# S5's pk products in 64 by 64 tiles over two PSUM banks, an early touch of pb, toe and kst, and a few reordered steps

## The chip, the cores and the metric

The kernel runs on one core of one Trainium2 chip. The metric is the device time of one execution in microseconds (us). Before the change the median of three runs is 1424.18 us (1423.64 to 1424.38). One execution was profiled; its own time and its span stand in the table further down.

TensorE (PE) does the matrix products, VectorE (DVE) and ScalarE (ACT) the elementwise work, GpSimd (POOL) a few small steps, SyncE (SP) issues the DMAs. SBUF is the working memory; PSUM, in eight banks, takes the products.

## The reference

One layer of a hybrid decoder on 256 prompt positions and 8 by 8 sample positions, so 320 columns in all, in float32. What matters here:

```
proj = rms_norm(x) @ w_in                      # S5 input u | q | k | v | g
s5:  x_t = lam_bar * x_{t-1} + B_bar u_t       # 64 groups of 16 channels, 64 complex states each
     y   = Re(C x) + d * u ;  y = gelu(y) ;  y * sigmoid(y @ w_glu + b)
ret: 8 heads of 128, rotary q and k, decay per head, chunked scan, norm per head, silu(g) gate
x = x + concat(s5, ret) @ w_out
x = x + (silu(h2 @ w_gate) * (h2 @ w_up)) @ w_ffn_out
```

The outputs are the two normed activations and the final S5 and retention states.

## The kernel before

**Dense products.** Every weight matrix is streamed from HBM in tiles of 8 blocks of 128 by 128 (`wload`, L122): an SP DMA fills `raw`, ACT casts it to `hi` (L133), DVE makes the rest `lo` (L135), three buffers each. `gemm` (L139) does three products for each block, hi by xhi, hi by xlo, lo by xhi (L145 to L147), each with 320 columns. The projections (`ps_p`) come first, then the output projections, the feed-forward part and a tail.

**Order.** PE and POOL run in the order in which the program is written down (`manual_schedule`, L944). That order comes from a planner: `clk.now` is moved on by a cost for each product (0.4 a block in `gemm`, the first argument of `mm` elsewhere), `spawn` puts a generator on a heap with a due time, and `run_due`, called between the blocks of a product, emits whatever is due. So the S5 and retention steps lie between the blocks of the projections. ACT, DVE and SP are put in order by the compiler's scheduler, by readiness and priority: weight loads come first (offset 3000), then evacuations of PSUM (`EVAC`, 1500), then the rest in program order. Once built, each engine and each DMA queue runs its list strictly in order.

**S5.** Eight chunks of 8 groups (`s5_chunk`, L578). A chunk c starts at planner time T0 + 32 c. It

- copies u into `up_`, writes it to DRAM (`via`, L586) and reads it back in another layout with eight SP DMAs into `kst` (L590), two buffers, so a chunk's eight wait until the chunk two before has used its buffer in `s5_outputs`;
- makes `cl0` (tile name `cz`), the C factors in a layout with blocks of zeros, with four ACT instructions (L597), `bl` and `cl` on DVE;
- 14.2 planner units later (`b1`) has PE transpose `bl` four times into `pt` (L625), which ACT copies to `bst`;
- 6.6 units later (`b2`) emits the outputs of the chunk before (`pending.pop()()`, L632: products `py` from `toe`, `kst`, `cl` and `xp`), then 16 products `pb` from `bst` and `kst` in 64 by 64 tiles, then the 8 products `pk_` from `bl` and `cl0` in 128 by 64 tiles (L645), written to columns 320 to 383 of the first of pb's two banks;
- copies pk to the last part of `toe` (L649), from where six SP DMAs (L654) make the other three parts of `toe`, and runs the scan (`s5_scan`).

A float32 product shows as two PE instructions in the profile. The tile form stands in its row, as 128\*128, 64\*64 or 128\*64 (rows by columns of the array).

**Retention, head 0.** `finish_norm` scales the rotary table and releases `s5_params2` (six DVE steps, L419), which waits behind the table's second product (`turned`, L997). `do_q` (L876) rotates q (`rot_`) and makes `qg` (two DVE products, L893). `do_k` (L900) rotates k. `head_k` transposes k, `head_v` transposes v, makes `vT`, copies a part of it to `vsp` (L770) and, for odd heads, uses it in `po`.

**Start.** POOL builds `ident`, then sets `ones` (L64), which eight warming products on PE use. 

Of the kernel before, what the change touches and what calls it, by code (L numbers as in the profile page):

```python
# [12 lines left out]
F32 = mybir.dt.float32  # L13
# [7 lines left out]
P = 128  # L21
# [11 lines left out]
CH = 4  # L33
NCP = NP // CH
NC = N // CH
# [11 lines left out]
def hybrid_kernel(ctx, tc, xT, w_in, w_in4, w_out, w_glu, w_fi, w_fo, w_fot, gfr, vecs, s5p, bc, x0,  # L47
# [11 lines left out]


    ident = cst.tile([P, P], F32, name="ident")
    make_identity(nc, ident)
    ones = cst.tile([P, P], F32, name="ones")
    pool.memset(ones, 1.0)  # L64
    mhalf = cst.tile([P, 4], F32, name="mhalf")
    pool.memset(mhalf, -0.5)
    vec = cst.tile([P, vecs.shape[1]], F32, name="vec")
# [251 lines left out]

    d0s = [s5.tile([P, 2, 4, NCP], F32, name=f"d0{i}") for i in range(2)]  # L320
    xps = [s5.tile([P, 2, 4, NC], F32, name=f"xp{i}") for i in range(2)]
    cl0s = [s5.tile([P, 2, 4, 32], F32, name=f"cz{i}") for i in range(2)]

    cls_ = [s5.tile([P, 2, 4, CH, 16], F32, name=f"cl{i}") for i in range(2)]


    toe = s5.tile([P, 4, CH, 16], F32, name="toe")
    for t_ in (*d0s, *xps, toe, *cl0s):
        pool.memset(t_, 0.0)
    scr = [None, 0]  # L330

# [245 lines left out]
    def s5_chunk(c):  # L577
        js = slice(4 * c, 4 * c + 4)  # L578
        cl, cl0, xp, d0 = cls_[c % 2], cl0s[c % 2], xps[c % 2], d0s[c % 2]

        up_ = s5.tile([P, CH, NC], F32, name="up_", tag="up_", bufs=2)
        with tc.issue_after(rot_t["keys"].ins) if c < 2 else nullcontext():
            act.copy(up_, u32[:, c].rearrange("p (c s) -> p s c", s=CH))

        via = drm.tile([4, 2, 16, CH, NC], F32, name="via", tag="via", bufs=2)
        sp.dma_start(via.rearrange("j g h s c -> (j g h) (s c)"), up_.rearrange("p s c -> p (s c)"))  # L586
        kst = s5.tile([P, 4, NC], F32, name="kst", tag="kst", bufs=2)
        for i in range(2):
            for e in range(CH):
                sp.dma_start(kst[64 * i + 16 * e:64 * i + 16 * e + 16],  # L590
                             via[2 * i:2 * i + 2, :, :, CH - 1 - e].rearrange("q g h c -> h (q g) c"))

        raw = raws[c]
        for q in range(2):
            for g in range(2):
                with tc.issue_after(rot_t["values"].ins):
                    act.mul(cl0[64 * g:64 * g + 64, q, :, 16 * g:16 * g + 16],  # L597
                            raw[64 * g:64 * g + 64, 1, 4 * q:4 * q + 4], 1.0 - 2.0 * q)
        with tc.issue_after(rot_t["values"].ins):
            act.copy(d0[:, :, :, 1:], r4[:, js].unsqueeze(1).unsqueeze(3).to_broadcast([P, 2, 4, NCP - 1]))  # L600
        shm = [P, 8, CH, 16]
        for w_, pc in ((0, gpc), (1, lpc)):
            m1, m2 = (s5.tile(shm, F32, name=f"m{q}", tag=f"m{q}", bufs=1) for q in range(2))
            b_ = raw[:, w_].unsqueeze(2).to_broadcast(shm)
            tt(m1, b_, pc[:, c, 0].unsqueeze(3).to_broadcast(shm), MUL)
            tt(m2, b_, pc[:, c, 1].unsqueeze(3).to_broadcast(shm), MUL)
            if w_ == 0:

                bl = s5.tile([P, 2, 2, 2, CH, 16], F32, name="bl", tag="bl", bufs=1)
                for r, (a, b, op) in enumerate(((m1[:, 0:4], m2[:, 4:8], SUB), (m1[:, 4:8], m2[:, 0:4], ADD))):  # L610
                    a, b = (t_.rearrange("p (u q) e h -> p u q (e h)", q=2) for t_ in (a, b))
                    tt(bl[:, r].rearrange("p q u e h -> p u q (e h)"), a, b, op)
                continue
            tt(cl[:, 0], m1[:, 0:4], m2[:, 4:8], SUB)
            tt(cl[:, 1], m1[:, 4:8], m2[:, 0:4], SUB)
        if c:
            tbl = s5_table(c)
        yield DL["b1"] + (4.0 if c == 0 else 0.0)
        if not c:
            tbl = s5_table(c)  # L620
        bst = s5.tile([P, 4, P], F32, name="bst", tag="bst", bufs=1)
        pt = misc("pt")
        for i in range(4):
            tr(pt[:, P * i:P * i + P], bl[:, i // 2, i % 2].rearrange("p u e h -> p (u e h)"))
        with tc.high_priority(offset=EVAC):  # L625
            act.copy(bst, pt.rearrange("p (i s) -> p i s", s=P))
        load_bc(c + 2)
        yield DL["b2"]
        if c:
            while clk.now - used["misc"] < MISC:  # L630
                yield 0.4
            pending.pop()()  # L632
        pb = ps_b.tile([P, 2, 512], F32, name="pb", tag="pb", bufs=1)
        for i in range(4):
            for u in range(2):

                for g in range(2):
                    us, gs = slice(64 * u, 64 * u + 64), slice(64 * g, 64 * g + 64)
                    mm(0.04, pb[gs, u, NC * i:NC * i + NC], bst[us, i, gs], kst[us, 2 * (i % 2) + g],
                       start=True, stop=True, tile_position=(64 * u, 64 * g))  # L640
        pk_ = pb[:, 0, 4 * NC:4 * NC + 64]
        for i in range(2):
            for q in range(2):
                for u in range(2):
                    mm(0.04, pk_[64 * u:64 * u + 64, 32 * i:32 * i + 32],  # L645
                       bl[:, q, i, u].rearrange("p e h -> p (e h)"), cl0[:, q, 2 * u + i],
                       start=q == 0, stop=q == 1, tile_position=(0, 64 * u))
        with tc.high_priority(offset=EVAC):
            act.copy(toe[:, :, CH - 1], pk_.rearrange("p (q h) -> p q h", h=16))  # L649
        with tc.high_priority(offset=4 * EVAC if c == 7 else 0):  # L650
            for u in range(2):
                for t in range(CH - 1):
                    d = 16 * (CH - 1 - t)
                    sp.dma_start(toe[64 * u + d:64 * u + 64, :, t], toe[64 * u:64 * u + 64 - d, :, CH - 1])  # L654
        with tc.high_priority(offset=2 * EVAC if c == 7 else 0):
            s5_scan(c, pb, xp, d0, tbl)
        if c < 7:
            pending.append(lambda: s5_outputs(c, kst, cl, xp))
            return
        yield DL["scan"]  # L660
        while clk.now - used["misc"] < MISC:
            yield 0.4
        s5_outputs(c, kst, cl, xp)
# [61 lines left out]
    def rot_(ps, name):  # L725
        sw = mp.tile([P, N], F32, name="sw", tag="sw", bufs=1)
        act.copy(sw[0:64], ps[64:128])
        rot_t["keys"] = act.copy(sw[64:128], ps[0:64])
        a = mp.tile([P, N], F32, name=name, tag=name, bufs=1)
        tt(a, ps, csr[:, 0], MUL)  # L730
        tt(sw, sw, csr[:, 1], MUL)
        tt(a, a, sw, ADD)
        return a

    def head_k(h, q_, qg, k_, R):
# [25 lines left out]
    def head_v(h, v_, qg, rt, R):  # L761
# [5 lines left out]
        with tc.high_priority(offset=EVAC):  # L767
            for i in range(3):
                act.mul(vT[:, i], pst2[:, P * i:P * i + P], rtok[:, i:i + 1])
        act.copy(vsp[64 * (h % 2):64 * (h % 2) + 64], vT[64:128, 2])  # L770
        last = act.copy(vs[:, h], vT[64:128, 2])
        if h == 0:
            rot_t["values"] = last
# [24 lines left out]
        with tc.high_priority(offset=GN):  # L798
            for i in range(nt):
                dve.bn_stats(st[:, i], po[:, i])  # L800
                dve.bn_aggr(mv[:, :, i], st[:, i])

        m_, t_, y_, w_ = mv[:, 0], mv[:, 1], y[:, 0], y[:, 1]
        pool.tensor_scalar(m_, m_, -1.0, None, MUL)
# [6 lines left out]
        pool.tensor_tensor(w_, m_, y_, MUL)  # L811
        if h == 0:
            rot_t["first"]()
        on = mp.tile([P, 3, P], F32, name="on", tag="on", bufs=1)

        def normed():
# [59 lines left out]
    def do_q(h, ps=None):  # L876
# [13 lines left out]
        q_ = rot(ps, "q_")  # L890
        pool.tensor_copy(qsp[:, 64 * (h % 2):64 * (h % 2) + 64], q_[:, NP:N])
        qg = qgs[h % 2]
        for u in range(2):  # L893
            tt(qg[:, u].rearrange("p (b w) -> p b w", w=40)[:, :, 0:NS],
               q_[:, NP + 32 * u:NP + 32 * u + 32].rearrange("p (b t) -> p b t", t=NS),
               gqt[:, h].unsqueeze(1).to_broadcast([P, 4, NS]), MUL)
        R.update(q_=q_, qg=qg)
        run_due()

    def do_k(h, ps=None):  # L900
        ps = proj(9 + 4 * h) if ps is None else ps
        R = HS[h]
        k_ = rot(ps, "k_")
        pool.tensor_tensor(kvf[:, h], k_[:, NP:N].rearrange("p (b t) -> p b t", t=NS),
                           kdt[:, h].unsqueeze(1).to_broadcast([P, NB, NS]), MUL)
        pool.tensor_copy(ksp[:, 64 * (h % 2):64 * (h % 2) + 64], k_[:, NP:N])
        spawn(head_k(h, R["q_"], R["qg"], k_, R))
        run_due()
# [80 lines left out]
    def finish_norm():  # L989
        next(rg)  # L990
        act.copy(rtok, ytok[0])
        yield 4.5
        rps = next(rg)
        with tc.high_priority(offset=EVAC):
            act.copy(rbc, rps)
            tt(csr[:, 0], csr[:, 0], rbc, MUL)
            turned = dve.tensor_tensor(csr[:, 1], csr[:, 1], rbc, MUL)  # L997
            tt(u32[:, 0], ps0, rbc, MUL)
            tt(u32[:, 1], ps1, rbc, MUL)
        rot_t["ready"] = True  # L1000

        with tc.issue_after(turned.ins):
            s5_params2(exps[1])

    spawn(finish_norm(), DL["nm"])

# [538 lines left out]
```

## Time and profile before

| what | value |
| --- | --- |
| median of three runs | 1424.18 us |
| profiled execution, its own time | 1424.95 us |
| its span, first to last instruction | 1423.2 us |
| ACT busy | 606.5 us (43%) |
| POOL busy | 122.8 us (9%) |
| HBM read and written | 254.44 MB and 10.52 MB |
| granted PE clock, mean | 0.999 |

The page of the profile lists busy time by engine, groups of instructions and the chain of work that ended last. Times in timelines are counted from the start of the span. A row of the timeline has start, length, engine, line, operation, the tile written and the tiles read, the form, and the number of like instructions merged in it; a bracket tells how long the engine was idle before it and what ended that. "SPq" is a DMA issue in SP's queue: its length is the issue, not the transfer. "PEld" is the loading of weights into the array.

### The profile page before, as it was taken

The page shows a single profiled execution, that of the slowest core. Times are in us where ns is not written, and L with a number is a line of the kernel's source. Part 1 is how long each engine was busy: PE and PEld are TensorE (multiplying, and loading weights), DVE is VectorE, ACT ScalarE, POOL GpSimd, SP SyncE. Part 2 cuts the span into 40 slices and gives each one's busy share as a digit, 9 for nine tenths or more (in the row PEclk, how much of TensorE's full clock was granted, in tenths as well). Part 3 has the DMA queues.
Part 4 walks back from the last instruction along what each step waited for, and adds up shares of the span by engine and source line. Part 5 has one row for each costly group of instructions (what it writes and reads, how often), then busy time and mean ns, then how long its engine had stood idle before and what let it go on. Part 6 is the DMA issues. An engine that isn't in the chain of part 4 may idle for free.

```text
span 1423.2 us, 26196 instructions
## 1 busy us (share of the span) xinstructions
PE 1415.5 (99%) x10376; PEld 1406.6 (99%) x10376; DVE 957.9 (67%) x1842; ACT 606.5 (43%) x973; POOL 122.8 (9%) x194
## 2 busy tenths in 40 slices
PE   9999999999999999999999999999999999999998
PEld 8999999999999999999999999999999999999998
DVE  7979878787557747777777545767644677655453
ACT  6654555555455443333333333333333333334553
POOL 7720111110000000100001000000000000000002
PEclk9999999999999999999999999999999999999999
DMA  8554555555644466675666446666545765445542
GB/s 278 170 187 158 163 174 157 171 163 157 218 156 151 164 209 228 221 253 201 245 206 231 136 148 238 233 216 235 170 146 175 255 233 190 159 157 184 154 143 75
DMA packets 102316, 267.07 MB, mean 188 GB/s; under 512 B 27377, under 2 KB 42033, under 8 KB 102193
## 3 DMA queue, kind: packets, MB, share of 16 engines
q1 hardware_dynamic: 101904, 265.01, 55.9%
q8 instruction: 81, 1.33, 0.4%
q10 hardware_dynamic: 288, 0.39, 0.1%
q14 instruction: 43, 0.34, 0.1%
HBM read 254.44 MB, written 10.52 MB: 186 GB/s over the span
## 4 chain that ended last, share of the span: by engine, by line
PE 96%; DVE 2%; DMA 1%; ACT 1%; issue 1%; POOL 0%; SPq 0%; POOLq 0%; DVEq 0%; ACTq 0%
PE ps_fg L147 7%; PE ps_fu L147 7%; PE ps_fu L146 7%; PE ps_fg L146 7%; PE ps_fg L145 7%; PE ps_fu L145 7%; PE ps_fo L147 7%; PE ps_fo L145 7%; PE ps_fo L146 7%; PE ps_p L145 6%; PE ps_p L147 6%; PE ps_p L146 6%; PE ps_o L145 2%; PE ps_o L146 2%; PE ps_o L147 2%; PE ps_t L1342 1%
## 5 line engine op out<-in xcount | busy, mean ns | idle before, releaser
L133 ACT CAST hi<-raw 128x1024 fp32r<-128x1024 f32 (+1 forms) x410 | 397.8, 971 | 684.2 <-PE ps_fg L146 182.3
L135 DVE TENSOR_TENSOR lo<-raw,hi 128x1024 fp32r<-128x1024 f32 (+1 forms) x410 | 462.8, 1129 | 304.2 <-ACT hi L133 301.3
L147 PE MATMUL ps_fg<-hhi,lo 128*128 128x320 f32 x704 | 218.0, 310 | 0.0
L147 PE MATMUL ps_fu<-hhi,lo 128*128 128x320 f32 x704 | 217.9, 310 | 0.0
L145 PE MATMUL ps_fg<-hhi,hi 128*128 128x320 f32 x704 | 217.9, 310 | 0.0
L146 PE MATMUL ps_fu<-hlo,hi 128*128 128x320 f32 x704 | 217.9, 310 | 0.0
L145 PE MATMUL ps_fu<-hhi,hi 128*128 128x320 f32 x704 | 217.9, 310 | 0.0
L146 PE MATMUL ps_fg<-hlo,hi 128*128 128x320 f32 x704 | 217.9, 310 | 0.0
L145 PE MATMUL ps_fo<-ahl,hi 128*128 128x320 f32 x671 | 208.0, 310 | 0.0
L147 PE MATMUL ps_fo<-ahl,lo 128*128 128x320 f32 x671 | 207.7, 310 | 0.0
L146 PE MATMUL ps_fo<-ahl,hi 128*128 128x320 f32 x671 | 207.7, 310 | 0.0
L145 PE MATMUL ps_p<-xhi,hi 128*128 128x320 f32 x560 | 177.3, 317 | 0.0
L147 PE MATMUL ps_p<-xhi,lo 128*128 128x320 f32 x560 | 173.3, 309 | 0.0
L146 PE MATMUL ps_p<-xlo,hi 128*128 128x320 f32 x560 | 173.1, 309 | 0.0
L147 PEld LDWEIGHTS ps_fg<-hhi,lo 128*128 128x128 f32 x704 | 132.2, 188 | 0.0
L146 PEld LDWEIGHTS ps_fu<-hlo,hi 128*128 128x128 f32 x704 | 132.2, 188 | 0.0
L146 PEld LDWEIGHTS ps_fg<-hlo,hi 128*128 128x128 f32 x704 | 132.2, 188 | 0.0
L145 PEld LDWEIGHTS ps_fg<-hhi,hi 128*128 128x128 f32 x704 | 132.2, 188 | 0.0
L147 PEld LDWEIGHTS ps_fu<-hhi,lo 128*128 128x128 f32 x704 | 132.1, 188 | 0.0
L145 PEld LDWEIGHTS ps_fu<-hhi,hi 128*128 128x128 f32 x704 | 132.1, 188 | 0.0
L146 PEld LDWEIGHTS ps_fo<-ahl,hi 128*128 128x128 f32 x671 | 126.0, 188 | 0.0
L147 PEld LDWEIGHTS ps_fo<-ahl,lo 128*128 128x128 f32 x671 | 126.0, 188 | 0.0
(476 smaller groups left out, 2117.8 us busy)
## 6 DMA issues: line engine op xcount, KB each, us to landing
raw<-w_fi SPq DMA_DIRECT2D x176, 512.0 KB, 4.2
raw<-w_in SPq DMA_DIRECT2D x79, 512.0 KB, 4.1
raw<-w_fo SPq DMA_DIRECT2D x61, 512.0 KB, 3.5
raw<-w_out SPq DMA_DIRECT2D x32, 512.0 KB, 3.7
hi<-vd SPq DMA_DIRECT2D x32, 512.0 KB, 5.4
lo<-vd SPq DMA_DIRECT2D x32, 512.0 KB, 5.2
raw<-w_fo SPq DMA_DIRECT2D x61, 192.0 KB, 2.4
rt<-r SPq DMA_DIRECT2D x8, 512.0 KB, 5.2
```

Of the source, the lines that this page charges most:

```text
L133: cast = act.copy(hi[:, :m], raw[:, :m])
L135: last_lo[0] = dve.tensor_tensor(lo[:, :m], raw[:, :m], f(hi[:, :m]), SUB)
L145: pe.matmul(ps, hi, xhi[:, k], start=k == 0, stop=False)
L146: pe.matmul(ps, hi, xlo[:, k], start=False, stop=False)
L147: pe.matmul(ps, lo, xhi[:, k], start=False, stop=k == nk - 1)
L1342: pe.matmul(ps[0:m, 0:TC], a3[:, x_, k, s:s + m], w_[:, k], start=k == 0 and x_ == 0 and w_ is whi, stop=k == FCT - 1 and w_ is wlo)
```

## The change

It has these parts. (1) The `pk` products read half of the rows each: 16 products of 64 rows, 64 columns of weights and 16 moving columns, in 64 by 64 tiles, row half g into bank g of `pb`; `cl0` loses its zero blocks and its memset, two ACT instructions make it in place of four, and the copy to `toe` reads both banks. (2) `pb` is allocated ahead of the transposes, and in chunks 1 to 7 a product of `toe` (three columns) and the first column of `kst` into one unused column of `pb` stands there. (3) The planner's costs follow, and chunk 7's outputs are due 1.2 later. (4) `s5_params2` waits behind the last step of q's rotation and is written down after k's; head 0's two `qg` products wait behind the statistics of head 0. (5) For odd heads the `vsp` copy has EVAC's priority. (6) DVE sets `ones`, first of all.

```diff
+    ones = cst.tile([P, P], F32, name="ones")
+    dve.memset(ones, 1.0)
     make_identity(nc, ident)
-    ones = cst.tile([P, P], F32, name="ones")
-    pool.memset(ones, 1.0)
...
-    cl0s = [s5.tile([P, 2, 4, 32], F32, name=f"cz{i}") for i in range(2)]
+    cl0s = [s5.tile([P, 2, 4, 16], F32, name=f"cz{i}") for i in range(2)]
...
-    for t_ in (*d0s, *xps, toe, *cl0s):
+    for t_ in (*d0s, *xps, toe):
...
         for q in range(2):
-            for g in range(2):
-                with tc.issue_after(rot_t["values"].ins):
-                    act.mul(cl0[64 * g:64 * g + 64, q, :, 16 * g:16 * g + 16],
-                            raw[64 * g:64 * g + 64, 1, 4 * q:4 * q + 4], 1.0 - 2.0 * q)
+            with tc.issue_after(rot_t["values"].ins):
+                act.mul(cl0[:, q], raw[:, 1, 4 * q:4 * q + 4], 1.0 - 2.0 * q)
...
         pt = misc("pt")
+        pb = ps_b.tile([P, 2, 512], F32, name="pb", tag="pb", bufs=1)
+        if c:
+            mm(0.06, pb[0:CH - 1, 1, 511:512], toe[:, 0, 0:CH - 1, 0], kst[:, 0, 0:1], start=True, stop=True)
         for i in range(4):
             tr(pt[:, P * i:P * i + P], bl[:, i // 2, i % 2].rearrange("p u e h -> p (u e h)"))
...
-        pb = ps_b.tile([P, 2, 512], F32, name="pb", tag="pb", bufs=1)
...
-        pk_ = pb[:, 0, 4 * NC:4 * NC + 64]
         for i in range(2):
             for q in range(2):
-                for u in range(2):
-                    mm(0.04, pk_[64 * u:64 * u + 64, 32 * i:32 * i + 32],
-                       bl[:, q, i, u].rearrange("p e h -> p (e h)"), cl0[:, q, 2 * u + i],
-                       start=q == 0, stop=q == 1, tile_position=(0, 64 * u))
+                for g in range(2):
+                    for u in range(2):
+                        gs, col = slice(64 * g, 64 * g + 64), 4 * NC + 16 * i
+                        mm(0.03, pb[64 * u:64 * u + 64, g, col:col + 16],
+                           bl[gs, q, i, u].rearrange("p e h -> p (e h)"), cl0[gs, q, 2 * u + i],
+                           start=q == 0, stop=q == 1, tile_position=(64 * g, 64 * u))
         with tc.high_priority(offset=EVAC):
-            act.copy(toe[:, :, CH - 1], pk_.rearrange("p (q h) -> p q h", h=16))
+            act.copy(toe[:, :, CH - 1].rearrange("p (i g) h -> p g i h", g=2),
+                     pb[:, :, 4 * NC:4 * NC + 32].rearrange("p g (i h) -> p g i h", h=16))
...
-        yield DL["scan"]
+        yield DL["scan"] + 1.2
...
-        act.copy(vsp[64 * (h % 2):64 * (h % 2) + 64], vT[64:128, 2])
+        with tc.high_priority(offset=EVAC if h % 2 else 0):
+            act.copy(vsp[64 * (h % 2):64 * (h % 2) + 64], vT[64:128, 2])
...
         if h == 0:
             rot_t["first"]()
+            with tc.issue_after(aggr.ins):
+                R["scaled_q"]()
...
+        R.update(q_=q_, qg=qg, scaled_q=scaled_q)
+        if h:
+            scaled_q()
...
         k_ = rot(ps, "k_")
+        if not h:
+            with tc.issue_after(rot_t["turned"].ins):
+                s5_params2(exps[1])
...
-        with tc.issue_after(turned.ins):
-            s5_params2(exps[1])
```

`scaled_q` holds the two `qg` products that `do_q` did before; `rot_t["turned"]` is now the last step of `rot_`.

More of the change, by code (lines that the diff above doesn't have):

```diff
@@ L731, in rot_ @@
         tt(sw, sw, csr[:, 1], MUL)
-        tt(a, a, sw, ADD)
+        rot_t["turned"] = dve.tensor_tensor(a, a, sw, ADD)
         return a
@@ L800, in head_v @@
                 dve.bn_stats(st[:, i], po[:, i])
-                dve.bn_aggr(mv[:, :, i], st[:, i])
+                aggr = dve.bn_aggr(mv[:, :, i], st[:, i])
         m_, t_, y_, w_ = mv[:, 0], mv[:, 1], y[:, 0], y[:, 1]
@@ L892, in do_q, with scaled_q @@
         qg = qgs[h % 2]
[L893 to L897, printed above, removed]
+        def scaled_q():
+            for u in range(2):
+                tt(qg[:, u].rearrange("p (b w) -> p b w", w=40)[:, :, 0:NS],
+                   q_[:, NP + 32 * u:NP + 32 * u + 32].rearrange("p (b t) -> p b t", t=NS),
+                   gqt[:, h].unsqueeze(1).to_broadcast([P, 4, NS]), MUL)
+        R.update(q_=q_, qg=qg, scaled_q=scaled_q)
+        if h:
+            scaled_q()
         run_due()
@@ L996, in finish_norm @@
             tt(csr[:, 0], csr[:, 0], rbc, MUL)
-            turned = dve.tensor_tensor(csr[:, 1], csr[:, 1], rbc, MUL)
+            tt(csr[:, 1], csr[:, 1], rbc, MUL)
             tt(u32[:, 0], ps0, rbc, MUL)
```

## The prediction

> **What bounds the kernel now.** First the page's busy times: they say which engine sets the end.
>
> ```profile
> span 1423.2 us, 26196 instructions
> ## 1 busy us (share of the span) xinstructions
> PE 1415.5 (99%) x10376; PEld 1406.6 (99%) x10376; DVE 957.9 (67%) x1842; ACT 606.5 (43%) x973; POOL 122.8 (9%) x194
> ```
>
> PE is busy for 1415.5 of 1423.2 us, in one stream written down by hand. So the time changes by what PE's stream gains or loses, and by nothing else: a faster ACT or DVE step counts only where PE waits for it, and a new wait in PE's stream counts in full, since nothing behind it can be taken forward and no slack follows to make it up. I read, in this order, the busy times, PE's waits, the PE timeline around an S5 chunk, and then SP's timeline at the places where the change lets PE ask for something earlier than before.
>
> **The early touch.** In chunks 1 to 7 a new product stands ahead of the four transposes into pt. It reads toe (written by the DMAs of the chunk before) and column 0 of this chunk's kst, over all 128 rows. Each of the chunk's eight kst DMAs writes 16 of those rows, so PE has to wait there for all eight. Before, the first reader of kst was the pb products, 6.6 planner units later. Here are the kst issues and pt of chunk 2, then of chunk 6.
>
> ```profile
> 142.32 0.90 SPq L590 DMA_DIRECT2D kst<-via  x2
> ...
> 144.68 0.60 PE L109 MATMUL pt<-ident,bl 128*128 128x128 f32 x4
> ...
> 148.65 0.35 SPq L132 DMA_DIRECT2D raw<-w_in  x1
> 149.04 0.43 SPq L590 DMA_DIRECT2D kst<-via  x1
> ...
> 153.35 0.88 PE L104 MATMUL pb<-kst,bst 64*64 64x80 f32 x32
> ...
> 284.06 0.90 SPq L590 DMA_DIRECT2D kst<-via  x2
> ...
> 286.55 0.60 PE L109 MATMUL pt<-ident,bl 128*128 128x128 f32 x4
> ...
> 287.10 0.35 SPq L132 DMA_DIRECT2D raw<-w_in  x1
> 287.49 1.37 SPq L590 DMA_DIRECT2D kst<-via  x3
> ```
>
> ```profile
> DMA to landing us min/median/max: 1.6/3.4/4.5
> ```
>
> The second fence is the time from issue to landing of all 64 kst DMAs. In chunk 2 the last of the eight is issued at 149.04 and, at the median 3.4, lands at 152.4: in time for pb at 153.35, but 7.8 us after pt at 144.68, where the touch now stands. In chunk 6 three are issued after pt; the last, about 0.42 before the end of 287.49 + 1.37, starts at 288.4, lands at 291.8, and so is 5.3 us late. The same two rows in each of the five chunks 2 to 6 (the first and the last are quoted) give 7.8, 1.9, 5.2, 5.4 and 5.3: 25.5 us. In chunk 1 the DMAs are long done and in chunk 7 they land just at pt, so I put 0 there.
>
> What decides is whether SP's list stays in this order. SP issues a chunk's kst between weight loads, and the load ahead of the last kst (148.65, 287.10) waits for a lo of DVE whose buffer PE freed before pt. So PE standing at the touch does not hold up that load, the list can stay as it is, and PE waits out the whole distance. If instead the scheduler puts the remaining kst DMAs straight behind the ones before, chunk 2's last is issued at 143.2 (142.32 + 0.90) and is late by 1.9, chunk 6's by 2.8 (284.06 + 0.90, two more issues, 3.4); reckoned so, the five sum to 11.0 us. That is the lower end. It cannot be below nothing, since no one needs kst earlier. I take 25.5, as all loads in between are of the kind just described. Queued behind the touch on PE are the transposes and every later weight product; ACT (bst, and the casts that wait for a freed hi buffer), then DVE and SP's next weight loads stand behind those.
>
> **The touch itself and the pk products.** PE around chunk 1:
>
> ```profile
> 119.78 0.73 PE L104 MATMUL py<-xp,cl 64*64 64x80 f32 x32
> 120.33 0.73 PE L104 MATMUL pb<-kst,bst 64*64 64x80 f32 x32
> 120.99 0.66 PE L104 MATMUL pb<-cz,bl 128*64 128x32 f32 x16
> 121.58 0.41 PE L145 MATMUL ps_p<-xhi,hi 128*128 128x320 f32 x1
> ```
>
> 32 instructions in 64 by 64 tiles take 0.55 us to the next start when the same form follows (119.78 to 120.33), and 0.66 when 128 by 64 follows: 0.11 for the change of form. The 16 of pk take 0.59, the change to 128 by 128 included. After the change pk is 32 instructions of the form that pb already has, so the 0.11 goes; the 32 take at most the 0.55 of those with five times the columns, and the change to 128 by 128 stays. I take a gain of 0.1 a chunk, 0.8 in all (ends 0 and 2.5, the latter with pk at half the pace of the 80-column rows).
>
> [...]
>
> The touch has three columns of weights, so it will run in a narrow form, between 128 by 128 products. The nearest rows are those of po, which go 128 by 128, 128 by 32 and back:
>
> ```profile
> 93.39 0.61 PE L104 MATMUL po<-vT,sm 128*128 128x128 f32 x4
> 93.84 0.39 PE L104 MATMUL po<-vsp,smp 128*128 128x128 f32 x2
> 94.16 1.08 PE L104 MATMUL po<-rt,qg 128*32 128x128 f32 x32
> 95.17 0.71 PE L104 MATMUL psr<-vT,kd 128*128 128x128 f32 x4
> 95.63 0.40 PE L145 MATMUL ps_p<-xhi,hi 128*128 128x320 f32 x1
> ```
>
> A pass is 0.1125 there (0.45 for four). The two ahead of the narrow ones take 0.32 instead of 0.225, the eight groups of four narrow ones 1.01 instead of 0.90: 0.2 for there and back, up to 0.1 more for the first pass after it. With the touch's own two passes I take 0.3, times seven 2.1 us (ends 1.4 and 3.2). Against it stands a gain: waits for kst and toe that now stand inside the 64 by 64 run go to the touch. Chunk 2's pb takes 0.88 where chunk 1's takes 0.73, so 0.15 in each of six chunks, 0.9 (ends 0 and 0.9).
>
> **Head 0.** PE's waits in the retention part, and the DVE steps that s5_params2 and qg are:
>
> ```profile
> PE pst L109 <- DVE k__737 L180: 0.3, 1, 0.3
> PE pst L109 <- ACT kd L743: 0.3, 1, 0.3
> ```
>
> ```profile
> 47.18 0.82 DVE L180 TENSOR_TENSOR lp<-rr,ecs 128x32 f32<-128x32 f32 x2
> ...
> 49.36 0.79 DVE L180 TENSOR_TENSOR qg<-q__727,gqt 128x32 f32<-128x32 f32 x2
> ...
> 52.71 0.34 DVE L428 RECIPROCAL scrt<-scrt 128x32 f32<-128x32 f32 x1
> ```
>
> These DVE steps stand inside q's and k's rotations, and PE waits twice, 0.3 each, for k. The edit takes up to 1.95 us of them out of the way, so the first wait should go; the second, for ACT's kd, goes only if ACT's list no longer has the gate's Silu ahead of kd. I take 0.5 of the 0.6 (ends 0 and 0.6). The moved qg steps fall where nobody waits: their reader is po of head 1, at 94.16.
>
> **The smaller edits.** One wait of PE for the vsp copy goes, 0.2 (the row below). Chunk 7's py from xp took 0.98 where chunk 1's took 0.73, as xp was late; with pb of chunk 7 a little earlier in PE's stream (the planner's costs grew) and the outputs due 1.2 later, I take 0.2 of it back (ends -0.3 and +0.3). DVE sets ones sooner, and the warming products start sooner, but the first real product waited for xhi, which waits for input from HBM: 0. What hides that is the gap between the two rows; without it it would be worth some 0.3. ACT's two saved instructions a chunk and the memset are off PE's path: 0.
>
> ```profile
>   ACT vsp L770: 0.2, 1
> ```
>
> ```profile
> 341.26 0.98 PE L104 MATMUL py<-xp,cl 64*64 64x80 f32 x32
> ```
>
> ```profile
> 1.12 3.47 PE L118 MATMUL warm_ps<-ones 128*128 128x512 f32 x8 [1.12 <-POOL ones L64]
> 5.11 0.38 PE L977 MATMUL py<-xhi,hi 128*128 128x320 f32 x1 [0.52 <-DVE xhi L180]
> ```
>
> **The sum.** Without the wait: -0.8 + 2.1 - 0.9 - 0.5 - 0.2 - 0.2 = -0.5. With it: 25.5 - 0.5 = +25.0 on the profiled execution, whose own time is 1424.95, or 1449.95; that execution lies 0.77 over the median 1424.18, so 1449.2 for a median.
>
> **The rivals.** *A, SP's list moves.* The scheduler, seeing PE stand at the touch, issues the remaining kst DMAs ahead of the loads: 11.0 - 0.5 - 0.77 + 1424.95 = 1434.7. For it: the loads that wait for PE's progress come later in such a list. Against: the loads named above do not. *B, no wait at all.* The kst DMAs are down before the touch, because other edits shift SP's list by two weight loads, or the touch does not carry the wait that I read into it; the change then does only its small things: 1423.7, from 1421 to 1426 by the ends of the small terms. It decides if the last kst issue lies 3.4 us ahead of pt in chunks 2 to 6. Against it: in all five it lies at most 1.5 us ahead, in four behind. *C, the clock falls in the waits.*
>
> ```profile
> 1420.70:1423.20 2.50, 0.00 (x0) 0.00 (x0) 0.00 (x0) 0.00 (x0) 0.00 (x0) 0.50 0.43 143
> ```
>
> In this row of the windows view the granted clock (0.50) is half, in the last 2.5 us, where PE has nothing left to do. Four of the five waits are longer than that. If each costs a stretch like the warm-up's 3.47 us at half the clock, PE loses 1.7 us each, 6.9 in all: 1456.1. [...]
>
> **How the numbers follow.** Chances: the forecast 0.42, A 0.22, C 0.18, B 0.18. The forecast, A and C hold 0.82, so the range goes from A's 1434.7 less the ends of the small terms and of the landing times, 1430, to C's 1456.1 plus some 3 for a planner shift that brings every pt 0.2 to 0.5 us earlier, 1459. The forecast's own range is 1444 to 1454. A measurement of this kernel can tell about 0.2%, 2.85 us, from no change. B gives 0.04 faster, 0.12 the same, 0.02 slower; all else is slower: 0.84.
>
> **What would show it.** PE's waits after the change would have a row of a new product (into pb, ahead of pt) waiting for DMA kst, five times, 2 to 8 us each, in chunks 2 to 6; SP's timeline would show each last kst issue behind a weight load; pk would stand in 64 by 64 form, with 64 by 64 before it and no step of 0.11; the waits for k and vsp would be gone. The granted clock around 150, 220, 255 and 290 would tell C. The forecast is wrong if PE shows no wait ahead of pt, or if the kst issues lie in front of the loads.

## The result and the profile after

After the change the median is 1461.58 us (1461.08 to 1462.92); the kernel before, run beside it, had 1423.97 (1423.64 to 1424.38). The ratio is 1.0265, 95% interval 1.0249 to 1.0282: 37.6 us slower. The measured time lies 12.4 us above the forecast of 1449.2 and 2.6 above the range's upper end. The profiled execution took 1462.92 with a span of 1461.1 us, 37.9 over the span before.

The page after: span, busy times, and the granted clock in 40 slices of 36.5 us.

```profile
span 1461.1 us, 26439 instructions
...
PE 1425.7 (98%) x10518; PEld 1416.4 (97%) x10518; DVE 959.2 (66%) x1843; ACT 603.2 (41%) x957; POOL 129.3 (9%) x191
...
PEclk9999899989999999999999999999999999999999
```

PE is busy 10.2 us longer with 142 instructions more, and idle for 27.7 us longer. The clock has two slices below nine tenths where it had none. PE's waits (line of the waiter, what it waited for: total, times, longest) say where the idle time is:

```profile
PE pb L104 <- DMA kst<-via: 20.9, 5, 6.5
PE pb L104 <- DMA via<-up__2368: 7.8, 1, 7.8
```

All of it stands at the touch, which is the only product into pb that reads toe. These are its rows in chunks 2 to 7, from PE's timeline; the bracket is the idle time ahead of it:

```profile
151.41 0.19 PE L104 MATMUL pb<-kst,toe 128*3 128x1 f32 x2 [7.85 <-DMA via<-up__2368]
...
193.05 0.19 PE L104 MATMUL pb<-kst,toe 128*3 128x1 f32 x2 [3.89 <-DMA kst<-via]
...
232.10 0.19 PE L104 MATMUL pb<-kst,toe 128*3 128x1 f32 x2 [2.56 <-DMA kst<-via]
...
273.20 0.19 PE L104 MATMUL pb<-kst,toe 128*3 128x1 f32 x2 [5.59 <-DMA kst<-via]
...
317.07 0.19 PE L104 MATMUL pb<-kst,toe 128*3 128x1 f32 x2 [6.49 <-DMA kst<-via]
...
357.20 0.19 PE L104 MATMUL pb<-kst,toe 128*3 128x1 f32 x2 [2.40 <-DMA kst<-via]
```

The six sum to 28.8 us. Chunk 2's wait is put down to the write of via, which the touch does not read; it is a DMA that stands behind the last kst in the same queue. SP's timeline shows the order:

```profile
138.07 2.06 SPq L590 DMA_DIRECT2D kst<-via  x3
140.95 0.35 SPq L132 DMA_DIRECT2D raw<-w_in  x1
141.35 0.90 SPq L590 DMA_DIRECT2D kst<-via  x2
147.13 0.35 SPq L132 DMA_DIRECT2D raw<-w_in  x1
147.53 0.43 SPq L590 DMA_DIRECT2D kst<-via  x1
...
148.94 0.46 SPq L586 DMA_DIRECT2D via<-up__2368  x1
```

The last kst, at 147.53, stands behind a weight load, and the touch starts 3.88 after it.

The other 9 us of the 37.9 are no waits. The windows view gives, for stretches of 3.41 us counted on from the clock's steps: length, busy time of PE, PEld, DVE, ACT and POOL, then the granted clock, the DMA share and GB/s.

```profile
142.36:145.77 3.41, 1.20 (x9) 0.94 (x7) 1.39 (x3) 2.82 (x6) 0.00 (x0) 1.00 0.40 144
145.77:149.18 3.41, 0.00 (x0) 0.00 (x0) 1.23 (x1) 0.08 (x1) 0.00 (x0) 0.50 0.29 96
149.18:152.60 3.42, 1.19 (x7) 1.19 (x8) 0.00 (x0) 0.00 (x0) 0.00 (x0) 0.50 0.64 207
152.60:156.01 3.41, 3.41 (x15) 3.41 (x14) 0.00 (x0) 0.59 (x1) 0.00 (x0) 0.50 0.00 0
156.01:159.42 3.41, 3.41 (x26) 3.41 (x25) 1.62 (x2) 1.05 (x1) 0.00 (x0) 1.00 0.00 0
...
227.69:231.10 3.41, 1.85 (x13) 1.58 (x12) 3.41 (x9) 1.62 (x3) 0.00 (x0) 1.00 0.58 172
231.10:234.52 3.42, 2.42 (x20) 2.41 (x21) 0.20 (x1) 0.97 (x3) 0.00 (x0) 1.00 0.72 221
...
316.44:319.85 3.41, 2.78 (x14) 2.78 (x15) 0.00 (x0) 1.46 (x4) 0.00 (x0) 0.50 0.01 3
319.85:323.26 3.41, 3.41 (x14) 3.41 (x14) 1.07 (x1) 2.39 (x6) 0.00 (x0) 0.50 0.00 0
...
353.98:357.39 3.41, 1.01 (x9) 0.75 (x8) 0.00 (x0) 0.51 (x2) 2.32 (x8) 1.00 0.48 147
357.39:360.81 3.42, 3.42 (x14) 3.42 (x15) 1.22 (x1) 2.07 (x4) 0.00 (x0) 0.50 0.00 0
```

The granted clock is 0.50 around five of the six waits, in whole stretches of 3.41 us (10.24, 3.41, 6.83, 10.24 and 3.41 us in all). After chunk 2's wait PE works at the halved clock from 151.41 to 156.01, where only 15 products fit into a stretch that takes 26 at full clock. PE's busy time in the eight stretches at half clock in which it works at all is 1.19 and 3.41 (chunk 2), 3.41 (3), 2.27 and 3.41 (5), 2.78 and 3.41 (6) and 3.42 (7): 23.3 us. The granted clock is 0.50 there, but the pace is a little better than half. These are neighbouring products at full clock, in chunk 1, and at half clock, behind chunk 3's wait:

```profile
117.80 0.31 PE L145 MATMUL ps_p<-xhi,hi 128*128 128x320 f32 x1
117.94 0.31 PE L146 MATMUL ps_p<-xlo,hi 128*128 128x320 f32 x1
...
194.03 0.47 PE L146 MATMUL ps_p<-xlo,hi 128*128 128x320 f32 x1
194.30 0.47 PE L147 MATMUL ps_p<-xhi,lo 128*128 128x320 f32 x1
```

From start to start the medians over all such neighbours are 0.147 and 0.267 us. So 45% of the 23.3 us is lost, 10.5 (half would be 11.65). Another way to the same number is the run with three kst buffers (below), which has the same PE list and neither these waits nor the falls: set against it product by product, after loses 2.0, 1.55, 0, 2.5, 2.8 and 1.55 us behind the touches of chunks 2 to 7, 10.4 in all. So 28.8 in waits, 10.5 in the clock, and the small parts give 1.4 back: 37.9.

### The profile page after: what moved, and what is told of

The parts are those of the page before. It is cut to its first block, busy times and chain, and to the rows that moved or that the text cites. A ratio compares the mean times of both kernels' runs of the same rounds, so it can differ in the third digit from the quotient of the medians.

```text
span 1461.1 us, 26439 instructions
## 1 busy us (share of the span) xinstructions
PE 1425.7 (98%) x10518; PEld 1416.4 (97%) x10518; DVE 959.2 (66%) x1843; ACT 603.2 (41%) x957; POOL 129.3 (9%) x191
## 4 chain that ended last, share of the span: by engine, by line
PE 89%; DVE 5%; DMA 2%; issue 1%; ACT 1%; POOL 1%; SPq 0%; POOLq 0%; DVEq 0%; ACTq 0%
PE ps_fu L146 7%; PE ps_fg L146 7%; PE ps_fg L147 7%; PE ps_fg L145 7%; PE ps_fu L147 7%; PE ps_fu L145 7%; PE ps_fo L145 7%; PE ps_fo L146 7%; PE ps_fo L147 7%; PE ps_p L145 4%; PE ps_p L146 4%; PE ps_p L147 4%; PE ps_o L145 2%; PE ps_o L147 2%; PE ps_o L146 2%; DVE lo L135 2%
## 5 line engine op out<-in xcount | busy, mean ns | idle before, releaser
L145 PE MATMUL ps_p<-xhi,hi 128*128 128x320 f32 x560 | 180.9, 323 | 0.0
L146 PE MATMUL ps_p<-xlo,hi 128*128 128x320 f32 x560 | 176.4, 315 | 0.0
L147 PE MATMUL ps_p<-xhi,lo 128*128 128x320 f32 x560 | 176.3, 315 | 0.0
L146 PEld LDWEIGHTS ps_fo<-ahl,hi 128*128 128x128 f32 x671 | 125.9, 188 | 0.0
L145 PEld LDWEIGHTS ps_fo<-ahl,hi 128*128 128x128 f32 x671 | 125.9, 188 | 0.0
```

What stands on the lines that cost most here:

```text
L145: pe.matmul(ps, hi, xhi[:, k], start=k == 0, stop=False)
L146: pe.matmul(ps, hi, xlo[:, k], start=False, stop=False)
L147: pe.matmul(ps, lo, xhi[:, k], start=False, stop=k == nk - 1)
```

## The experiments

Two questions were put. Is all of the loss in the touch's wait for kst, and what is kst late behind? Is the clock a loss of its own? My theory was that the touch waits for eight DMAs that SP issues too late, and that the clock falls in the waits on top; the rivals are named in the expectations. The median of the kernel before beside these runs lay between 1424.11 and 1424.47 us. "After" is the changed kernel.

### The touch taken out, and the touch on other data

```diff
-        if c:
-            mm(0.06, pb[0:CH - 1, 1, 511:512], toe[:, 0, 0:CH - 1, 0], kst[:, 0, 0:1], start=True, stop=True)
```

> The changed kernel without the one product of toe and kst ahead of the transposes; all else stays. Theory (PE waits at that product for the kst DMAs, and the clock falls in these waits): both go, and the small gains of the other parts are left, read from the profile after as pk 0.16 x 8 = 1.3, head 0 0.7, vsp 0.2, chunk 7's py 0.4: 1424.0 - 2.6 = 1421.4 us (1420.5 to 1422.5). No wait of PE for kst, no fall of the granted clock before the tail. Rival 1 (the pk products in 64 by 64 tiles over two banks, or pb's early allocation, make PE wait): it stays near 1461.

Measured: 1422.47 us, ratio to before 0.9986 (0.9977 to 0.9995), span 1420.1, no wait of PE on a DMA and no half clock ahead of the end. The whole loss hangs on this one product; all other edits together bring some 2 us, just clear of no change.

In the second run the product stays in its place and reads a column of `ones` in place of `kst`:

```diff
-                  ..., toe[:, 0, 0:CH - 1, 0], kst[:, 0, 0:1], ...
+                  ..., toe[:, 0, 0:CH - 1, 0], ones[:, 0:1], ...
```

> The product ahead of the transposes stays, but its moving column is of ones and not of kst, so it waits for toe and pb alone. Theory: no wait, since toe lands some 5 us ahead; the product and its two changes of form cost 0.27 us in each of seven chunks, 1.9, less some 0.4 for the waits for toe that leave the 64 by 64 run: about 1.5 over the kernel without it, 1423 us (1421.5 to 1424.5). Rival 2 (the wait is for toe's DMAs or for pb's last readers): it stays near 1461.

Measured: 1423.96, ratio 0.9999 (0.999 to 1.0008), and no wait at the touch. So it is the reading of kst, not the product or its place, and toe alone is in time. The difference to the run without the product, 1.5 us, is near the 1.9 that the rows give for seven such products (0.27 each, see below), but the two intervals overlap.

### The touch alone, in the kernel before

> The kernel before with the product of toe and kst alone, pk and all else as before. Theory: waits of about 28 us in chunks 2 to 7, 11 us lost to the half clock, 1 us for the product itself less the waits taken out of the 64 by 64 run: 1424 + 40 = 1464 us (1456 to 1472). Rival 1: it stays within a few us of 1424.

The edit is the three new lines of part (2) of the change, the allocation and the touch, and nothing else. Measured: 1461.24, ratio 1.0261 (1.0247 to 1.0275): the loss of the whole change, to 0.4 us. Its five waits of note sum to some 27 us, with five falls of the clock. This run also has the two stretches that lie nearest to each other on the two sides of the clock's fall:

```profile
190.19:193.60 3.41, 1.51 (x13) 1.48 (x13) 0.00 (x0) 0.55 (x2) 2.27 (x8) 1.00 0.79 185
193.60:197.02 3.42, 3.42 (x15) 3.42 (x14) 1.23 (x1) 2.03 (x4) 0.00 (x0) 0.50 0.88 347
313.07:316.48 3.41, 1.53 (x12) 1.29 (x10) 2.12 (x3) 3.13 (x8) 0.00 (x0) 1.00 0.38 131
316.48:319.89 3.41, 0.00 (x0) 0.00 (x0) 0.00 (x0) 0.00 (x0) 0.00 (x0) 1.00 0.77 206
319.89:323.31 3.42, 2.86 (x13) 2.85 (x14) 0.00 (x0) 0.84 (x2) 0.00 (x0) 0.50 0.01 2
```

Behind the stretch with 1.51 us of PE's work the next one ran at half clock, behind that with 1.53 the clock stayed full. The wait in the first of them is 1.90 us long, so here the clock fell with a wait shorter than any of the six in the changed kernel (2.40 at the least). After the last row, with 2.86 us of work at half clock, the clock is full again.

### The waits filled with products

```diff
+        for _ in range((0, 0, 33, 17, 11, 24, 28, 10)[c]):
+            pe.matmul(pb[:, 1], onesr, onesr.unsqueeze(1).to_broadcast([P, 4, P]), start=True, stop=True)
         if c:
             mm(0.06, pb[0:CH - 1, 1, 511:512], toe[:, 0, 0:CH - 1, 0], kst[:, 0, 0:1], start=True, stop=True)
```

The kernel is after with throwaway products of `ones` ahead of the touch, so many in each chunk as fill its wait. They keep PE busy and take nothing of the lateness away.

> The changed kernel with throwaway products of ones (512 columns, into pb's second bank) ahead of the product of toe and kst in chunks 2 to 7: 33, 17, 11, 24, 28 and 10 of them, about as long at full clock (0.235 us each, 28.9 us in all) as the waits were. Theory: PE is busy where it stood, so the granted clock stays at 1.00, the waits shrink to under 1 us each, and the 11.6 us lost to the half clock come back: 1450 us (1447 to 1455). Rival 3 (the falls of the clock do not come from PE standing idle, or cost nothing): 1461 or more.

Measured: 1453.15, ratio 1.0202 (1.0189 to 1.0216), mean clock 0.999. Chunk 2 in PE's timeline:

```profile
143.10 7.67 PE L623 MATMUL pb<-ones 128*128 128x512 f32 x33
151.24 0.19 PE L104 MATMUL pb<-kst,toe 128*3 128x1 f32 x2 [0.47 <-DMA via<-up__2401]
151.36 0.66 PE L109 MATMUL pt<-ident,bl 128*128 128x128 f32 x4
```

The touch starts at the same time as in after (151.24 and 151.41), with the wait full of products, and the four transposes behind it take 0.66 instead of the 1.12 that they take at half clock. No stretch at half clock is left ahead of the end. The median is 8.4 us below after's; the spans of the two profiled executions, the longest of after's four and the shortest of these four, lie 10.4 apart (1461.1 and 1450.7). The rows of after gave 10.5; the 11.6 of the expectation took the pace at half clock for half. So the clock is a loss of its own, of about the size read from the rows; what is left over the kernel with no touch is the lateness of kst.

### kst issued first

```diff
-        for i in range(2):
+        with tc.high_priority(offset=3500):
+          for i in range(2):
```

The eight kst DMAs get a priority over the weight loads'. If they are late only because they stand behind these, the loss goes.

> The changed kernel, the product of toe and kst in its place, with the eight kst DMAs of each chunk given priority over the weight loads in SP's list. Theory (the wait is there because SP issues kst behind weight loads): each chunk's kst is issued as soon as its buffer is free, some 20 us ahead of the product, the waits for kst and the falls of the clock go: about the 1424 us of the kernel whose product reads no kst (1422 to 1427; some us may go to weight loads that come later for it). Rival (the wait is for something else, or the product itself is slow): 1461.

Measured: 1463.09, ratio 1.0273 (1.0259 to 1.0287). The loss stayed whole, and the theory as it stood then failed. SP's timeline and PE's waits of this run:

```profile
118.78 4.64 SPq L591 DMA_DIRECT2D kst<-via  x8
...
143.72 1.24 SPq L657 DMA_DIRECT2D toe<-toe  x2
145.06 0.54 SPq L132 DMA_DIRECT2D raw<-w_in  x1
145.65 1.89 SPq L657 DMA_DIRECT2D toe<-toe  x3
```

```profile
PE pb L104 <- DMA toe<-toe: 17.3, 4, 5.6
PE pb L104 <- DMA raw_bc<-bc: 7.7, 1, 7.7
PE pb L104 <- DMA via<-up__3370: 5.3, 1, 5.3
```

kst is down early, as wanted, and now it is toe, the other tile that the touch reads, whose last three DMAs go out at 145.65. Between pb of one chunk and pt of the next SP has eight kst, six toe and eight yc DMAs to issue, between weight loads. What is taken forward there pushes something else back, and the touch waits for whichever of its two tiles stands last. That leads to the next run: the same, with a slice of `ident` in place of toe, so that the touch reads kst alone.

```diff
-                  ..., toe[:, 0, 0:CH - 1, 0], kst[:, 0, 0:1], ...
+                  ..., ident[:, 0:CH - 1], kst[:, 0, 0:1], ...
```

> As e5_kst_first (kst's DMAs ahead of the weight loads), but the touch multiplies a slice of ident with kst, so that it reads kst alone and no longer toe. Revised theory (the touch waits for whichever of toe and kst stands last in SP's list between two pb; with kst first and toe not read by it nothing is late): the waits at the touch are under 1 us in all, no clock fall, 1424 us, 1421 to 1428. Rival 1 (the kst DMAs, not toe, land late even when they are first): as after, 1455 to 1465. Rival 2 (toe is late also for the pt product that follows the touch, so that the wait moves from the touch to the next reader of toe): one wait a chunk stays after the touch, 1440 to 1463.

Measured: 1424.62, ratio 1.0002 (0.9992 to 1.0011), with no wait at the touch:

```profile
142.88 0.19 PE L104 MATMUL pb<-kst,ident 128*3 128x1 f32 x2
143.00 0.65 PE L109 MATMUL pt<-ident,bl 128*128 128x128 f32 x4
```

Its toe goes out as late as in the run before (the last three from 145.59), but its next reader, the py products, comes late enough. So in each of the two lists one of the two tiles is late for pt, kst in the one and toe in the other, and a product at pt that reads the late one waits. A product of kst alone in the list as it was has not been run; after's own waits, which are for kst, say that it would wait. Whether moving the eight kst DMAs ahead costs something by itself is open: this run is 1.9 us above the run with three buffers (below), in which the touch does not wait either, and that is within what noise can make.

### A third buffer for kst, and the touch later

```diff
-        kst = s5.tile([P, 4, NC], F32, name="kst", tag="kst", bufs=2)
+        kst = s5.tile([P, 4, NC], F32, name="kst", tag="kst", bufs=3)
```

> The changed kernel with three kst buffers in place of two, so a chunk's kst need not wait for the outputs two chunks before; priorities as they were. Theory: if the freeing of the buffer is what holds kst back, the waits shrink to nothing and the time comes to 1423 to 1425 us; if it is the place behind back, yc and toe in SP's list, which have the earlier place in the program, part of the waits stay: 1425 to 1461, and the row of PE's waits for kst tells how much.

Measured: 1422.69, ratio 0.9991 (0.9982 to 1.0), no wait at the touch. Chunk 2's kst now need not wait for the buffer's readers around 118; the first go out at 94.96 and the last two here, more than 30 us ahead of its touch at 142.63:

```profile
109.90 0.90 SPq L590 DMA_DIRECT2D kst<-via  x2
```

In the last run of this kind the allocation of pb stays where the change put it, and the touch alone stands after the transposes, just ahead of `pending.pop()()`:

> The product of toe and kst moved from ahead of the transposes to just ahead of the outputs of the chunk before, 6.6 planner units later, where kst was needed anyway. Theory: kst is down by then (in the kernel before its first reader there did not wait), so no wait and no fall of the clock; the product costs 0.15 to 0.27 in each of seven chunks and takes the waits for kst and toe out of the 64 by 64 run, 0.15 in each of six: within 1 us of the kernel without the product, 1422 to 1423.5. Rival (the product is slow wherever it stands): over 1426.

Measured: 1421.81, ratio 0.9984 (0.9975 to 0.9993), with 0.2 us of waits at the touch in all. 6.6 planner units later the same DMAs are down. The span is 40.4 us below after's with every edit of the change in it. The rows of after gave 28.8 + 10.5 = 39.3 for the waits and the clock. The other 1.1 fits the touch's own cost: here it stands between a projection product and the 64 by 64 products of py, where a change of form is due anyway (the next start comes 0.24 after that of the projection product with the touch and without it), and adds 0.12 (118.07 to 118.19) instead of 0.27, in each of seven chunks.

### The pk products alone, and the rest alone

The first is the kernel before with the new pk products, `cl0` and the copy to toe alone; the second is the change without these, without the touch and without the later due time of chunk 7's outputs, which neither of the two has.

> The kernel before with the new pk products alone (64 by 64 tiles, two banks, cl0 without zero blocks, two ACT instructions, the planner's cost of them), without the product of toe and kst and without the other edits. Theory: 0.16 us less in each of eight chunks, 1.3: ratio 0.9991, 1423.1 us where before has 1424.4; the planner's shift may bring chunk 7's outputs sooner and cost up to 0.4. Rival (twice as many passes cost more): 1425 to 1428.

> All edits of the change but the new pk and the touch: ones on VectorE, pb allocated early in chunk 0, the parameters and scaled_q moved, vsp with priority. Theory (these edits are worth what the rows of head 0 show, 0.7 us, and the gone wait for vsp, 0.2): 0.9 us under the kernel before, ratio about 0.9994. Rival (head 0's waits are a matter of the list's order, as the run with pk alone lost them without these edits, and come back or move elsewhere): within 0.3 us of the kernel before. Either lies at or inside what can be told from no change, so that the profile's rows of head 0 decide more than the time.

Measured: pk alone 1422.02, ratio 0.9986 (0.9977 to 0.9995); the rest alone 1424.02, ratio 0.9997 (0.9988 to 1.0006). So pk is a gain that can just be told from none, and the rest is not told from none. The rows of head 0 don't divide the gain in the same way: with pk alone, too, PE no longer waits for k, though none of head 0's steps was edited.

```profile
52.67 0.38 PE L109 MATMUL pst<-ident,k__735 128*128 128x128 f32 x2
...
54.06 0.39 PE L145 MATMUL ps_p<-xhi,hi 128*128 128x320 f32 x1
```

From k's transposes to the next projection product are 1.39 us here, 1.40 with the rest alone and, from the end of the wait, 1.63 before (with a second wait, for kd, inside). ACT has two instructions fewer in each chunk in this run, and the scheduler's lists differ; which of the two takes the waits away was not tried apart. The wait for vsp is gone with pk alone as well, and chunk 7's py from xp take 0.73 there without the later due time, where the rest alone leaves them at 0.98, as before. So none of these gains needs parts (4) and (5) of the change or the later due time, to which the prediction put them down for the most part. The two gains, 2.1 and 0.4 us, come to what the run without the touch gains, about 2, within the intervals.

## Why the prediction was wrong in size

The direction and the mechanism were right: PE stands at the touch in chunks 2 to 6, kst is the reason, the last kst issue stands behind a weight load (147.13 and 147.53), and nothing behind PE makes it up. On the profiled execution 1449.95 was forecast and 1462.92 measured, 13.0 more: 10.5 of them are the clock, which stood at nothing in the sum, 3.3 are the waits, and the small parts gave 0.9 more back than forecast. So two terms failed by their size, and SP's list was read too simply.

**The clock.** The step that failed most is that the fall of the clock was set apart as rival C, with a chance of 0.18, and stood at nothing in the forecast's sum; and rival C's price, "a stretch like the warm-up's 3.47 us at half the clock, PE loses 1.7 us each" in four waits, 6.9, was too low. The granted clock fell around five waits and took 10.5 us, 2.1 each. Each of them cost a stretch at half clock, that in which PE resumed or, in chunks 3 and 7, that which began 0.51 and 0.19 us later; behind the waits of chunks 2, 5 and 6, where it held 1.19, 2.27 and 2.78 us of work, the next one ran at half clock too: chunks 3 and 7 lost 1.55, near the price, but chunk 2 lost 2.0, chunk 5 2.5 and chunk 6 2.8. With 25.5 + 10.5 - 0.5 - 0.77 on 1424.95 the forecast would have been 1459.7. The filled waits show that this loss is the clock's and not the wait's. That the warm-up ran at half the clock is seen in its pace alone: its eight products of 512 columns took 0.43 us each (3.47 in all), the throwaway products of the same form 0.23 (7.67 for 33); the trace of before records no granted clock until 4.10 us.

The length of the wait alone did not tell where the clock fell: it fell at chunk 7's wait of 2.40 us and not at chunk 4's longer one of 2.56. The five falls of after begin at 145.77, 193.56, 272.06, 313.02 and 357.39 us. Chunk 7's wait (354.80 to 357.20) lay within one of the stretches of 3.41 us, with 1.01 us of work in it, chunk 4's (229.54 to 232.10) across two, with 1.85 and 2.42.

**The waits.** Forecast 7.8, 1.9, 5.2, 5.4, 5.3 and 0 for chunks 2 to 7, 25.5 in all; measured 7.85, 3.89, 2.56, 5.59, 6.49 and 2.40, 28.8. Chunk 7 was put at nothing, on a landing "just at pt"; that is a margin of nothing, not a wait of nothing. The landing after the last issue was taken at the median of all 64 DMAs, 3.4, where chunk 2 needed 3.88. And in chunks 3 and 4 the list was not the old one to the microsecond (+2.0 and -2.6); by what, was not tried. That the sum is only 3.3 off is in part luck: chunk 4's -2.6 stands against chunk 7's +2.4.

**SP's list.** The reason that I gave for the lateness, weight loads ahead of kst, holds for this kernel but is not what has to be mended: with kst ahead of the loads toe took its place, and the time stayed at 1463.09. Between pb and the next pt the list holds the chunk's 22 small DMAs among weight loads, and SP stands at those: from 60 to 370 us of after its weight loads wait 123.1 us, in 45 waits, for lo of DVE. In both lists the last of the late tile's DMAs go out behind such a load (147.13 and 147.53 in after, 145.06 and 145.65 with kst first). A list in which none of the 22 stands behind a weight load was not tried. Rival A, that the list moves in the change's favour, fell in chunk 2 by its rows; rival B, no wait, fell throughout.

**The small parts.** -0.5 was forecast; 28.8 in waits and 10.5 in the clock leave -1.4 of the measured 37.9. In the rows after:

```profile
118.33 0.51 PE L104 MATMUL py<-kst,toe 64*64 64x80 f32 x16
118.66 0.73 PE L104 MATMUL py<-xp,cl 64*64 64x80 f32 x32
119.21 0.73 PE L104 MATMUL pb<-kst,bst 64*64 64x80 f32 x32
119.76 0.60 PE L104 MATMUL pb<-cz,bl 64*64 64x16 f32 x32
120.30 0.41 PE L145 MATMUL ps_p<-xhi,hi 128*128 128x320 f32 x1
```

pb and pk take 1.09 us (119.21 to 120.30) instead of 1.25: 0.16 a chunk, 1.3 in all where I had 0.8. The change of form is gone, as forecast: from pb to pk are 0.55 (119.21 to 119.76) where 0.66 stood. The 32 passes of pk take 0.54 with the change to 128 by 128 in them, about the 0.55 that those with five times the columns take without it: single starts in the trace show that groups of four passes follow each other by 0.058 us with 16 columns and by 0.069 with 80. The runs of 64 by 64 products over all chunks, in which the waits for kst stood before, lose 2.1 us, these 1.3 and 0.8 of waits (0.9 forecast). The touch costs 0.27 where it does not wait, 1.9 for seven (2.1 forecast). Head 0 gains 0.74, from 2.28 to 1.54 us between the projection products (0.5 forecast), the wait for vsp is gone (0.2), and chunk 7's outputs take 0.99 instead of 1.38 (0.2 forecast). These make -1.5, about the -1.4 that is left.

## What to carry to other kernels

A product moved ahead in an engine's fixed order brings its reads forward with it: look for every DMA that writes what it reads, and when the last of them is issued, before counting it as a small instruction; giving one tile's DMAs priority only helps if the product's other tile does not take their place. A wait in a busy PE stream can have a second price beside its length, the clock: here five of six waits had it, and it came to over a third of their length (10.5 us on 28.8). What was useful in this change, pk in 64 by 64 tiles and the reordered steps, is worth 0.16% with the touch further back (1421.81 us, the lowest median here, though not told from pk alone, 1422.02), and the touch itself is not needed for it.

## What the runs showed of the hardware

- In after the granted clock stood at 0.50 for 10.24, 3.41, 6.83, 10.24 and 3.41 us, in or less than 0.6 us behind the waits of 7.85, 3.89, 5.59, 6.49 and 2.40 us, and at 1.00 around that of 2.56. In after and touch alone the stretches of 3.41 us just ahead of their ten falls, that at the end left aside, held 0 to 1.51 us of PE's work; the one with 1.53 (touch alone, 313.07 to 316.48) had no fall behind it. At 0.50, the stretch with 2.78 us of work (after, 316.44 to 319.85) was followed by another at 0.50, the one with 2.86 (touch alone, 319.89 to 323.31) by full clock. What sets the clock was not tried.
- At a granted clock of 0.50 the products of 320 columns followed each other by 0.267 us in after, instead of 0.147 at 1.00: 1.8 times as long, not twice.
- A fifth of the columns saved little in 64 by 64 tiles: in after, groups of four passes follow each other by 0.058 us with 16 columns (pk) and by 0.069 with 80 (pb).
- The touch, a product with three columns of weights between 128 by 128 products, cost 0.27 us in chunk 1, where it did not wait: it takes 0.12 to the next start, it stands 0.24 behind a projection product, where such products follow each other by 0.147, and the transposes behind it take 0.41 to the next product instead of the 0.35 without it.
